# Sums of cached rows in one decoder step: 32 small matmuls a batch on TensorE in place of multiply-adds on VectorE and GpSimd

## The chip, the cores and the metric

The program runs on one core of one Trainium2 chip. The metric is the device time of one execution in microseconds (us), as the median of several runs. Engines are called TensorE (PE in the rows, with PEld for its weight loads), VectorE (DVE), ScalarE (ACT), GpSimd (POOL) and SyncE (SP, which here only issues transfers).

## What is computed

One inference step of a one-layer hybrid decoder, for a prompt of 512 tokens and for 8 sequences that decode 4 tokens each. The step has modulation vectors, an input projection, attention in three branches, a state-space mixer (SSD), an output projection and a mixture of 16 experts. The change concerns one piece of the attention of the 8 decoding sequences: 2048 cached key and value rows of each sequence are compressed, 32 rows to one, with one weight for each position.

```
def compress(rows, w_pos):
    b, l, g, d = rows.shape
    return jnp.einsum('bcjgd,j->bcgd', rows.reshape(b, l // CMP_BLOCK, CMP_BLOCK, g, d), w_pos)

rows = cache_cmp[layer, page_table].reshape(bd, PAST_LEN, 2, N_KV, HEAD_DIM)
kcmp = rmsnorm(compress(rows[:, :, 0], w_pos_k), g_k_cmp)
vcmp = compress(rows[:, :, 1], w_pos_v)
```

CMP_BLOCK is 32, a row has 128 numbers of key and 128 of value, and a sequence has 64 compressed rows.

## The kernel before

A sequence (a "batch" below, 0 to 7) is fetched by two gathers of 1 MB, `gcmp`, each of 128 partitions with 8 consecutive rows: four neighbouring partitions hold one block of 32 rows. `pool_batch(b)` makes the weighted sum over the 8 rows of a partition, the keys by one ScalarE and seven VectorE instructions (lines 492 and 494) and the values by four GpSimd instructions (lines 496 to 499), into the tile `psum` (an ordinary tile; the name is short for partial sums). Then TensorE adds each four partitions with the 0/1 mask `PM` in four matmuls, which write 32 PSUM partitions each, and ScalarE copies the result to `kvc`.

The eight batches are fillers among other work of the first part of the program, in an order written out by hand: `ORDER = "C f1 p f3 z c0 f1 c1 f4 q f1 c2 f2 c3 f1 e B f2"`. Here `fN` takes the next N fillers, which alternate `pool_batch(n)` and `ada_block(n + 4)` (32 small matmuls of the modulation vectors from 2 MB of weights, and 4 for a bias), and one `pool_batch` stands ahead of the list. C, z, q and B are quarters of the input projection; each is a loop over eight slices k in which ScalarE makes `wh` (line 339), VectorE makes `wl` (line 340) and TensorE runs 12 matmuls into the four `acc` tiles. `c0` to `c3` are the chunks of the SSD scan, with a chain of ScalarE (`lh`, `dec`), VectorE (`dec`, line 649) and TensorE; `p` is its convolution on VectorE (`ts`, lines 605 to 610).

The order on each engine is that of the framework's scheduler, which starts from the program's order and from its own estimate of when operands are ready; each engine then works its list strictly from the front. All gathers and 1 MB weight slices (`wada`, `wC`, `wF`, `wA`, `wB`) share seven slots (`SLOT`), so that a transfer starts when the reader of an earlier tile is done. SyncE issues the weight loads, GpSimd's queue the gathers. All matmuls are issued by the helper at line 97, so that their rows have this line and are told apart by their tiles.

Of the kernel before, what the change touches and what calls it, by code (L numbers as in the profile page):

```python
# [9 lines left out]
F32 = mybir.dt.float32  # L10
# [3 lines left out]
AF = mybir.ActivationFunctionType  # L14
OP = mybir.AluOpType
AX = mybir.AxisListType

P = 128
# [37 lines left out]
def hybrid_step(ctx: ExitStack, tc: tile.TileContext, a, o):  # L56
    nc = tc.nc
    V, S, G, T, SP = nc.vector, nc.scalar, nc.gpsimd, nc.tensor, nc.sync
# [7 lines left out]
    def nm(base):  # L66
        cnt[0] += 1
        return f"{base}_{cnt[0]}"

    def pool(name, side=None):  # L70
        cm = tc.tile_pool(name=name, bufs=1, reuse_waits="tile", side=side)
        p = cm.__enter__()
        return p, lambda: cm.__exit__(None, None, None)

    def const(shape, dt, name):
        return cst.tile(list(shape), dt, name=name, tag=name)

    def W(pl, shape, dt, tag, bufs=2):
        return pl.tile(list(shape), dt, name=nm(tag), tag=tag, bufs=bufs)

    psum = {}
# [8 lines left out]
    def PS(tag="ps"):  # L90
        return psum["pool"].tile([P, 512], F32, name=nm(tag), tag=tag, bufs=psum["tags"][tag])

    def SLOT(shape, dt=F32, name="st"):
        return st.tile(list(shape), dt, name=nm(name), tag="st8")

    def mm(out, lhsT, rhs, start=True, stop=True):
        T.matmul(out, lhsT, rhs, start=start, stop=stop)  # L97
# [83 lines left out]
    p1, close_p1 = pool("p1")  # L181
    ph, close_ph = pool("ph", "right")
# [52 lines left out]
    def brow(name, n, ap=None):  # L235
        t = const([P, n], F32, "bc_" + name)
        SP.dma_start(t, dram(a[name], 0, ap or [[0, P], [1, n]]))
        return t
# [23 lines left out]
    def block_mask(t, pattern, w, base=0):  # L262
        G.memset(t, 1.0)
        G.affine_select(t, t, pattern=pattern, compare_op=OP.is_ge, fill=0.0, base=base, channel_multiplier=1)
        G.affine_select(t, t, pattern=[[-s, n] for s, n in pattern], compare_op=OP.is_ge, fill=0.0,
                        base=w - 1 - base, channel_multiplier=-1)
# [19 lines left out]
    for k in range(KC):  # L286
        ps = PS("acc")
# [151 lines left out]
    with tc.issue_after(load_D(3)):  # L439
# [4 lines left out]
        wk8, wv8 = [brow(name, 8, [[0, 32], [8, 4], [1, 8]]) for name in ("w_pos_k", "w_pos_v")]  # L444
# [20 lines left out]
    ps = PS()  # L465
# [17 lines left out]

    def pool_batch(b):

        sums = W(ph, [P, 2, 256], F32, "psum")
        for h in range(2):
            gt = SLOT([P, 8, 256], name="gcmp")
            G.indirect_dma_start(out=gt.rearrange("p r c -> p (r c)"), out_offset=None, in_=cmp_rows,
                                 in_offset=bass.IndirectOffsetOnAxis(ap=idx[:, 2 * b + h:2 * b + h + 1], axis=0))  # L490
            y = sums[:, h, 0:P]
            S.activation(y, gt[:, 0, 0:P], AF.Copy, scale=wk8[:, 0:1])  # L492
            for i in range(1, 8):
                V.scalar_tensor_tensor(y, gt[:, i, 0:P], wk8[:, i:i + 1], y, op0=OP.mult, op1=OP.add)  # L494
            gv = gt[:, :, P:256]
            G.tensor_mul(gv, gv, wv8[:, :, None].to_broadcast([P, 8, P]))  # L496
            G.tensor_add(gv[:, 0:4, :], gv[:, 0:4, :], gv[:, 4:8, :])
            G.tensor_add(gv[:, 0:2, :], gv[:, 0:2, :], gv[:, 2:4, :])
            G.tensor_add(sums[:, h, P:256], gv[:, 0, :], gv[:, 1, :])
        ps = PS()  # L500
        for kv in range(2):
            for h in range(2):
                q = 32 * (2 * kv + h)
                mm(ps[q:q + 32, 0:P], PM, sums[:, h, kv * P:(kv + 1) * P])
        S.copy(kvc[:, b, :], ps[:, 0:P])


    PM = const([P, 32], F32, "PM")
    block_mask(PM, [[-4, 32]], 4)
    Wp = W(p1, [P, 2, NT, 16], F32, "Wp", 1)  # L510
    block_mask(Wp[:, 0], [[128, NT], [-32, 16]], 32)
    V.tensor_scalar_mul(Wp[:, 1], Wp[:, 0], wkp[:, 1:2])
    V.tensor_scalar_mul(Wp[:, 0], Wp[:, 0], wkp[:, 0:1])

    fillers = [f for n in range(8) for f in ((pool_batch, n), (ada_block, n + 4))]

    def fill(n):
# [7 lines left out]
    gts = mid.tile([P, NT, 32], F32, name="gts")  # L525
# [3 lines left out]
    ps = [PS(), PS()]  # L529
# [315 lines left out]
    for i, src in enumerate((us[:, 768:896], us[:, 1024:1152], kcv[:, 0:P])):  # L845
# [3 lines left out]
                        op=OP.add)  # L849
# [24 lines left out]
    ps = PS("sm")  # L874
# [13 lines left out]
    for t in range(NT):  # L888
# [6 lines left out]
        for hf in range(2):  # L895
            ps = PS("s")
# [59 lines left out]
    ps = PS("sm")  # L956
# [165 lines left out]
    ps = PS("sm")  # L1122
# [4 lines left out]
    ps = PS("sm")  # L1127
# [21 lines left out]
    ps = PS("sm")  # L1149
# [8 lines left out]
    for hb in range(2):  # L1158
        ps = PS("sm")
# [25 lines left out]
    ps = PS("sm")  # L1185
# [32 lines left out]
    ps = [PS("sm"), PS("sm")]  # L1218
# [17 lines left out]
    ps = [PS("sm"), PS("sm")]  # L1236
# [13 lines left out]
    for b2 in range(4):  # L1250
        ps = PS("sm")
# [28 lines left out]
    for g in range(2):  # L1280
# [7 lines left out]
                    op=OP.mult)  # L1288
# [23 lines left out]
    for i in range(4):  # L1312
        ph = PS("sm")
# [25 lines left out]
    ps = PS("s")  # L1339
# [9 lines left out]
    ps = PS("s")  # L1349
# [14 lines left out]
    for h in range(8):  # L1364
        for j in range(2):
            mm(pcs, kcT[:, h // 4, j, 112 - 16 * h:240 - 16 * h], QT[:, h, :], start=h == 0 and j == 0,
               stop=h == 7 and j == 1)
# [21 lines left out]
    ps = PS("s")  # L1389
# [4 lines left out]
    for t in range(NT):  # L1394
        ps = PS("s")
# [97 lines left out]
    for k in ko:  # L1493
        src = att if k < 4 else zy
        kk = k % 4
        ps = PS()
# [5 lines left out]
    ps = PS("pr")  # L1502
# [9 lines left out]
    ps = PS("pr")  # L1512
    for k in range(KC):
        T.transpose(ps[:, 32 * k:32 * k + 32], atS[:, k // 4, (k % 4) * P:(k % 4 + 1) * P], ident[0:NS, 0:NS])
    V.tensor_tensor(catS, ps[:, 0:256].rearrange("p (k c) -> p k c", c=NS), gcat[:, :, None].to_broadcast([P, KC, NS]),
                    op=OP.mult)
# [50 lines left out]
    ps = PS()  # L1567
# [8 lines left out]
    ps = PS()  # L1576
# [89 lines left out]
    ps = PS()  # L1666
# [97 lines left out]
    ps = PS()  # L1764
# [257 lines left out]
    with tc.issue_after(first), tc.issue_after(placed):  # L2022
        ps = PS("rt")
# [16 lines left out]
    with tc.issue_after(X[2]):  # L2040
        rts = {}
        for e in SEQ:
            ps = PS("rt")
# [8 lines left out]
    for i in range(NE + 1):  # L2052
        with tc.issue_after(X[3]):
# [4 lines left out]
            if n <= NE and n not in rts and n != XPOS:  # L2058
                ps = PS("rt")
# [54 lines left out]
def build(nc, shapes):  # L2114
    a, o = {}, {}
    for name in _INS:
        shape, dt = shapes[name]
        a[name] = nc.dram_tensor("in_" + name, shape, dt, kind="ExternalInput").ap()
    for name, shape in _OUTS:
        o[name] = nc.dram_tensor("out_" + name, shape, F32, kind="ExternalOutput").ap()  # L2120
    with tile.TileContext(nc, schedule_with_timeline_sim=True) as tc:
        hybrid_step(tc, a, o)
# [11 lines left out]
```

## Time and profile before

| | |
|---|---|
| median of 3 runs | 886.49 us (886.35 to 887.79) |
| profiled execution | 883.6 us, its span 881.9 us |
| TensorE busy in the span | 739.2 us (84%) |
| VectorE | 652.9 us (74%) |
| ScalarE | 394.3 us (45%) |
| GpSimd | 335.4 us (38%) |
| mean granted clock of TensorE | 0.903 of full |

The profiled execution has 1.7 us outside its span, and lies 2.9 us under the median. In rows of TensorE one f32 matmul leaves two records. A granted clock of 1.00 is 2.4 GHz, 0.50 is 1.2 GHz; a value between them is a mean over a stretch. The eight batches lie between 67 and 293 us of the span.

### The profile page before, as it was taken

The page shows a single profiled execution, that of the slowest core. Times are in us where ns is not written, and L with a number is a line of the kernel's source. Part 1 is how long each engine was busy: PE and PEld are TensorE (multiplying, and loading weights), DVE is VectorE, ACT ScalarE, POOL GpSimd, SP SyncE. Part 2 cuts the span into 40 slices and gives each one's busy share as a digit, 9 for nine tenths or more (in the row PEclk, how much of TensorE's full clock was granted, in tenths as well). Part 3 has the DMA queues.
Part 4 walks back from the last instruction along what each step waited for, and adds up shares of the span by engine and source line. Part 5 has one row for each costly group of instructions (what it writes and reads, how often), then busy time and mean ns, then how long its engine had stood idle before and what let it go on. Part 6 is the DMA issues. An engine that isn't in the chain of part 4 may idle for free.

```text
span 881.9 us, 14660 instructions
## 1 busy us (share of the span) xinstructions
PE 739.2 (84%) x5315; PEld 530.5 (60%) x5315; DVE 652.9 (74%) x1481; ACT 394.3 (45%) x894; POOL 335.4 (38%) x304
## 2 busy tenths in 40 slices
PE   5998868489969769998898898899589788898893
PEld 4666645376647555565557556677566557666662
DVE  5536899666795885745546645769899979989994
ACT  4324232332523423455244235422357557777781
POOL 1115565535481641100101301522335435466552
PEclk9999889779889759999999689999589989999997
DMA  8977474355641551113525032898388976876411
GB/s 290 376 227 278 149 282 166 144 191 188 242 144 48 194 207 53 44 44 149 191 100 191 1 96 82 262 338 312 122 319 279 286 239 212 282 235 210 115 32 21
DMA packets 67095, 161.85 MB, mean 184 GB/s; under 512 B 19005, under 2 KB 31238, under 8 KB 60622
## 3 DMA queue, kind: packets, MB, share of 16 engines
q1 hardware_dynamic: 56798, 115.54, 38.3%
q0 software_dynamic: 10224, 45.37, 15.7%
q8 instruction: 42, 0.69, 0.3%
q14 instruction: 31, 0.25, 0.1%
HBM read 153.48 MB, written 20.74 MB: 198 GB/s over the span
## 4 chain that ended last, share of the span: by engine, by line
PE 46%; DVE 32%; DMA 11%; issue 5%; ACT 4%; POOL 1%; SPq 1%; POOLq 0%; DVEq 0%; ACTq 0%
PE acc L97 16%; DVE wl L340 8%; PE smo L97 5%; DVE psum L494 4%; PE ps L97 4%; PE s L97 3%; DMA gcmp<-in_cache_cmp,idx 3%; PE sm L1008 3%; PE ot L97 3%; PE pt L805 3%; PE sm L97 2%; DMA gu<-in_w_up 2%; DMA wada<-in_w_ada 2%; DVE XL L1884 1%; DVE ts L607 1%
## 5 line engine op out<-in xcount | busy, mean ns | idle before, releaser
L494 DVE SCALAR_TENSOR_TENSOR psum<-gcmp,bc_w_pos_k,psum 128x128 f32<-128x128 f32 x112 | 62.9, 566 | 15.0 <-ACT psum L492 13.3
L97 PE MATMUL acc<-wl,XH 128*128 128x512 f32 x136 | 60.1, 442 | 11.5 <-DVE wl L340 7.7
L97 PE MATMUL acc<-wl,hH 128*128 128x512 f32 (+1 forms) x128 | 54.5, 429 | 18.1 <-DVE wl L340 18.1
L339 ACT CAST wh<-gu 128x512 fp32r<-128x512 f32 x88 | 51.3, 623 | 14.5 <-PE acc L97 12.1
L97 PE MATMUL acc<-wh,XH 128*128 128x512 f32 x136 | 55.4, 408 | 0.4 <-ACT XH L1883 0.4
L97 PE MATMUL acc<-wh,XL 128*128 128x512 f32 x136 | 54.8, 403 | 0.7 <-DVE XL L1884 0.7
L340 DVE TENSOR_TENSOR wl<-gu,wh 128x512 fp32r<-128x512 f32 x66 | 51.6, 812 | 1.0 <-ACT wh L339 0.9
L97 PE MATMUL acc<-wh,hL 128*128 128x512 f32 (+1 forms) x128 | 52.1, 410 | 0.0
L802 ACT ACTIVATE psb<-s,amx 128x128 f32<-128x128 f32 (+3 forms) x64 | 33.8, 528 | 40.7 <-DVE amx L800 33.1
L1032 POOL DMA_INDIRECT gsel<-in_cache_sel,idx x16 | 16.8, 1052 | 88.7 <-PE smo L97 75.5
L800 DVE TENSOR_REDUCE amx<-s 128x1 f32<-128x128 f32 (+3 forms) x64 | 30.8, 483 | 19.8 <-PE s L97 11.2
L97 PE MATMUL acc<-wh,hH 128*128 128x512 f32 (+1 forms) x128 | 43.5, 416 | 2.3 <-ACT wh L339 2.2
L97 PEld LDWEIGHTS acc<-wl,hH 128*128 128x128 f32 x128 | 27.5, 214 | 26.0 <-DVE wl L340 20.0
L340 DVE TENSOR_TENSOR wl<-dn,wh 128x512 fp32r<-128x512 f32 x39 | 38.3, 1001 | 5.8 <-ACT wh L339 5.7
L97 PEld LDWEIGHTS acc<-wl,XH 128*128 128x128 f32 x136 | 26.3, 194 | 25.8 <-DVE wl L340 15.5
L340 POOL TENSOR_TENSOR wl<-gu,wh 128x512 fp32r<-128x512 f32 x22 | 31.3, 1458 | 21.7 <-ACT wh L339 21.6
L97 PE MATMUL s<-KT,QT 128*128 128x384 f32 (+3 forms) x128 | 38.2, 384 | 1.1 <-DVE qa L823 0.8
L1929 POOL DMA_INDIRECT out_y_prompt<-yo,gir x16 | 28.3, 1770 | 26.5 <-DVE yo L1923 8.3
L97 PE MATMUL ps<-wada,scT 128*32 128x128 f32 x768 | 37.1, 280 | 1.1 <-DMA wada<-in_w_ada 0.5
L805 PE MATMUL pt<-ident,psb 128*128 128x128 f32 x160 | 32.4, 305 | 6.0 <-ACT psb L802 5.9
L339 ACT CAST wh<-dn 128x512 fp32r<-128x512 f32 x52 | 31.8, 620 | 12.1 <-PE acc L97 10.7
L496 POOL TENSOR_TENSOR gcmp<-gcmp,bc_w_pos_v 128x1024 f32<-128x1024 f32 x16 | 31.7, 1982 | 12.8 <-DMA gcmp<-in_cache_cmp,idx 12.8
(790 smaller groups left out, 2177.7 us busy)
## 6 DMA issues: line engine op xcount, KB each, us to landing
wada<-in_w_ada SPq DMA_DIRECT2D x24, 1024.0 KB
dn<-in_w_down SPq DMA_DIRECT2D x12, 1024.0 KB
gu<-in_w_gate SPq DMA_DIRECT2D x21, 512.0 KB
gu<-in_w_up SPq DMA_DIRECT2D x21, 512.0 KB
gux<-in_w_gate SPq DMA_DIRECT2D x11, 512.0 KB
gux<-in_w_up SPq DMA_DIRECT2D x11, 512.0 KB
wt<-in_cache_win SPq DMA_DIRECT2D x4, 1024.0 KB
wout<-in_w_out SPq DMA_DIRECT2D x4, 1024.0 KB
```

Of the source, the lines that this page charges most:

```text
L97: T.matmul(out, lhsT, rhs, start=start, stop=stop)
L339: S.copy(wh[:, 0:n], w)
L340: (eng or V).tensor_sub(wl[:, 0:n], w, wh[:, 0:n].bitcast(F32))
L494: V.scalar_tensor_tensor(y, gt[:, i, 0:P], wk8[:, i:i + 1], y, op0=OP.mult, op1=OP.add)
L496: G.tensor_mul(gv, gv, wv8[:, :, None].to_broadcast([P, 8, P]))
L607: V.scalar_tensor_tensor(c, xpad[:, k, j:j + 512], cwT[:, j, k:k + 1], c, op0=OP.mult, op1=OP.add)
L800: V.tensor_reduce(mx, ps[:, 0:n], axis=AX.X, op=OP.max, negate=True)
L802: S.activation(pb[:, 0:n], ps[:, 0:n], AF.Exp, bias=mx, accum_out=sm[:, h:h + 1])
L805: T.transpose(pt[:, c * P:(c + 1) * P], pb[:, c * P:(c + 1) * P], ident)
L1008: T.transpose(ps[:, j * P:(j + 1) * P], src(j), ident)
L1032: G.indirect_dma_start(out=t.rearrange("p r c -> p (r c)"), out_offset=None, in_=sel_rows, in_offset=bass.IndirectOffsetOnAxis(ap=idx[:, 2 ...
L1929: G.indirect_dma_start(out=y_p, out_offset=bass.IndirectOffsetOnAxis(ap=gi, axis=0), in_=yo, in_offset=None, bounds_check=511, oob_is_err= ...
```

## The change

`pool_batch` no longer makes sums on VectorE and GpSimd. Sixteen masks `PW` are made once: `PM` times the weight of row i, for keys and for values. For each batch TensorE multiplies each of the 8 rows of a partition with its mask and accumulates in PSUM: 8 rows by keys and values by two gathers are 32 matmuls where there were 4. Both gathers of a batch are issued ahead of its first matmul, and both slots are held until its last. Nothing else is edited, and GpSimd keeps only the gathers' issues of this work.

```
     def pool_batch(b):
 
-        sums = W(ph, [P, 2, 256], F32, "psum")
+        gts = []
         for h in range(2):
             gt = SLOT([P, 8, 256], name="gcmp")
             G.indirect_dma_start(out=gt.rearrange("p r c -> p (r c)"), out_offset=None, in_=cmp_rows,
                                  in_offset=bass.IndirectOffsetOnAxis(ap=idx[:, 2 * b + h:2 * b + h + 1], axis=0))
-            y = sums[:, h, 0:P]
-            S.activation(y, gt[:, 0, 0:P], AF.Copy, scale=wk8[:, 0:1])
-            for i in range(1, 8):
-                V.scalar_tensor_tensor(y, gt[:, i, 0:P], wk8[:, i:i + 1], y, op0=OP.mult, op1=OP.add)
-            gv = gt[:, :, P:256]
-            G.tensor_mul(gv, gv, wv8[:, :, None].to_broadcast([P, 8, P]))
-            G.tensor_add(gv[:, 0:4, :], gv[:, 0:4, :], gv[:, 4:8, :])
-            G.tensor_add(gv[:, 0:2, :], gv[:, 0:2, :], gv[:, 2:4, :])
-            G.tensor_add(sums[:, h, P:256], gv[:, 0, :], gv[:, 1, :])
+            gts.append(gt)
         ps = PS()
-        for kv in range(2):
-            for h in range(2):
-                q = 32 * (2 * kv + h)
-                mm(ps[q:q + 32, 0:P], PM, sums[:, h, kv * P:(kv + 1) * P])
+        for i in range(8):
+            for kv in range(2):
+                for h in range(2):
+                    q = 32 * (2 * kv + h)
+                    mm(ps[q:q + 32, 0:P], PW[:, kv, i, :], gts[h][:, i, kv * P:(kv + 1) * P], start=i == 0, stop=i == 7)
         S.copy(kvc[:, b, :], ps[:, 0:P])
...
     block_mask(PM, [[-4, 32]], 4)
+    PW = W(p1, [P, 2, 8, 32], F32, "PW", 1)
+    for kv, w8 in enumerate((wk8, wv8)):
+        V.tensor_tensor(PW[:, kv], PM[:, None, :].to_broadcast([P, 8, 32]), w8[:, :, None].to_broadcast([P, 8, 32]),
+                        op=OP.mult)
```

The scheduler orders the changed program anew. The first place is TensorE's list in the projection q, where batch 5 is to be summed. The matmuls into the four `acc` tiles are full ones with 128 output partitions, and those into `ps` write 32 partitions and belong to the batch. Before:

```order
L97 MATMUL acc_1908<-wh_2013,hH 128x512
L97 MATMUL acc_1908<-wl_2014,hH 128x512
L97 MATMUL acc_1908<-wh_2013,hL 128x512
L97 MATMUL acc_1909<-wh_2013,hH 128x512
L97 MATMUL ps_2141<-psum_2112,PM 32x128 x2
L97 MATMUL acc_1909<-wl_2014,hH 128x512
L97 MATMUL acc_1909<-wh_2013,hL 128x512
L97 MATMUL acc_1910<-wh_2013,hH 128x512
```

The same place in TensorE's list after the change:

```order
L97 MATMUL acc_1926<-wh_2011,hH 128x512
L97 MATMUL ps_2134<-gcmp_2130,PW_837 32x128
L97 MATMUL acc_1926<-wl_2012,hH 128x512
L97 MATMUL ps_2134<-gcmp_2132,PW_837 32x128
L97 MATMUL acc_1926<-wh_2011,hL 128x512
L97 MATMUL ps_2134<-gcmp_2130,PW_837 32x128
L97 MATMUL acc_1927<-wh_2011,hH 128x512
L97 MATMUL ps_2134<-gcmp_2132,PW_837 32x128
L97 MATMUL acc_1927<-wl_2012,hH 128x512
```

Where two small matmuls stood between full ones in a pair, single small ones now alternate with full ones. Between 75 and 296 us of the span before, and in the same part of the program after, 52 small matmuls stand alone between full ones where 5 did, and the runs of small matmuls between full ones number 83 where there were 39; the other batches stand in blocks.

The second place is GpSimd's list after the first batch: the gathers (line 489), the window norms (line 552 before, 549 after) and the sums. Before:

```order
L489 DMA gcmp_1311<-in_cache_cmp,idx 128x2048
L489 DMA gcmp_1325<-in_cache_cmp,idx 128x2048
L499 TENSOR_TENSOR psum_1233<-gcmp_1248 128x128
L496 TENSOR_TENSOR gcmp_1311<-gcmp_1311,bc_w_pos_v 128x8x128
L552 TENSOR_TENSOR wino<-wino,bc_g_k_win 128x4x64 x2
L489 DMA gcmp_1751<-in_cache_cmp,idx 128x2048
L497 TENSOR_TENSOR gcmp_1311<-gcmp_1311 128x4x128
L498 TENSOR_TENSOR gcmp_1311<-gcmp_1311 128x2x128
```

GpSimd's list at the same gathers after the change:

```order
L489 DMA gcmp_1241<-in_cache_cmp,idx 128x2048
L489 DMA gcmp_1319<-in_cache_cmp,idx 128x2048
L489 DMA gcmp_1321<-in_cache_cmp,idx 128x2048
L549 TENSOR_TENSOR wino<-wino,bc_g_k_win 128x4x64 x2
L489 DMA gcmp_1762<-in_cache_cmp,idx 128x2048
L489 DMA gcmp_1764<-in_cache_cmp,idx 128x2048
L651 TENSOR_TENSOR xdw_1604<-xt_1534,bc_d_skip 128x512
```

The gathers no longer stand behind sums of an earlier gather, so that only the release of a slot holds them. That release now comes from TensorE: in SyncE's list the first slice of `wA`, which is issued into a slot of batch 3, waited for VectorE, ScalarE and GpSimd before, and waits for TensorE after.

## Rows read from the trace of the kernel before

**Rows 1.** The page: busy us (share) x instructions of each engine.

```profile
PE 739.2 (84%) x5315; PEld 530.5 (60%) x5315; DVE 652.9 (74%) x1481; ACT 394.3 (45%) x894; POOL 335.4 (38%) x304
```

**Rows 2.** Chain of work that ended last, 75 to 296 us, shares by line.

```profile
by line: PE acc L97 18.8%; DVE psum L494 17.8%; DMA gcmp<-in_cache_cmp,idx 13.2%; PE ps L97 10.9%; DVE ts L607 5.1%; DVE wl L340 4.9%; issue 3.8%; DVE dec L649 3.6%; DVE qa L718 2.6%; DVE sp_mp L155 1.6%; DVE ts L605 1.5%; DVE rsq_yk L119 1
```

**Rows 3.** 75 to 296 us: length, busy of PE, PEld, DVE, ACT, POOL; clock; DMA.

```profile
75.00:296.00 221.00, 178.75 (x1526) 132.31 (x1524) 176.35 (x338) 73.09 (x196) 121.94 (x108) 0.88 0.47 170
```

**Rows 4.** Waits of TensorE, 75 to 296 us: us in total, times, longest.

```profile
PE acc L97 <- DVE wl L340: 19.1, 7, 8.7
PE ps L97 <- DVE dec L649: 14.1, 3, 11.1
PE ps L97 <- DVE psum L494: 3.3, 2, 1.9
```

**Rows 5.** Tile `gcmp`: duration ns min/median/max, first and last start.

```profile
L494 DVE SCALAR_TENSOR_TENSOR psum<-gcmp,bc_w_pos_k,psum x112: 246/351/2635, 75.8 to 270.2; 128x128 f32<-128x128 f32 x112
...
L496 POOL TENSOR_TENSOR gcmp<-gcmp,bc_w_pos_v x16: 1894/1939/2417, 75.4 to 256.6; 128x1024 f32<-128x1024 f32 x16
L497 POOL TENSOR_TENSOR gcmp<-gcmp x16: 1262/1284/2401, 77.4 to 259.7; 128x512 f32<-128x512 f32 x16
```

**Rows 6.** Stretch: length, busy of PE and PEld on tile `wada`, clock.

```profile
206.40:208.50 2.10, 1.96 (x64) 1.69 (x64) 1.00 0.00 0
```

**Rows 7.** The page, costliest groups: small matmuls of `wada`, mean 280 ns.

```profile
L97 PE MATMUL ps<-wada,scT 128*32 128x128 f32 x768 | 37.1, 280 | 1.1 <-DMA wada<-in_w_ada 0.5
```

**Rows 8.** Timeline of TensorE, start and duration us: small matmuls between full ones.

```profile
138.72 0.39 PE L97 MATMUL acc<-wl,hH 128*128 128x512 f32 x1
138.96 0.39 PE L97 MATMUL acc<-wh,hL 128*128 128x512 f32 x1
139.27 0.41 PE L97 MATMUL ps<-wF,hsT 128*32 128x128 f32 x4
139.62 0.33 PE L623 MATMUL ps<-ident,xx 128*128 128x128 f32 x1
...
217.28 0.41 PE L97 MATMUL ps<-wA,hsT 128*32 128x128 f32 x2
217.61 0.39 PE L97 MATMUL ps<-dta,LT 128*128 128x8 f32 x2
```

**Rows 9.** Stretches of 2 us: first and last of 35 with clock under 0.99.

```profile
82.00:84.00 2.00, 1.57 (x10) 0.88 (x9) 1.97 (x4) 1.96 (x5) 1.60 (x2) 0.87 0.00 0
...
266.00:268.00 2.00, 2.00 (x7) 1.57 (x6) 1.08 (x5) 0.22 (x1) 0.00 (x0) 0.55 0.60 122
```

**Rows 10.** Timeline of TensorE: idle before it and its releaser in brackets.

```profile
124.70 0.80 PE L97 MATMUL acc<-wl,hH 128*128 128x512 f32 x1 [4.69 <-DVE wl L340]
172.00 0.69 PE L97 MATMUL ps<-xt,dec 128*128 128x64 f32 x2 [11.14 <-DVE dec L649]
263.97 0.79 PE L97 MATMUL acc<-wl,hH 128*128 128x512 f32 x1 [8.70 <-DVE wl L340]
```

**Rows 11.** Chain of work that ended last: start us, us, what.

```profile
67.44 7.89 DMA gcmp<-in_cache_cmp,idx
...
155.54 8.59 DMA gcmp<-in_cache_cmp,idx
...
243.43 6.96 DMA gcmp<-in_cache_cmp,idx
...
256.95 5.83 DVE qa L718 x4
```

**Rows 12.** Timeline of SyncE: the first issue of `wA`.

```profile
178.99 0.90 SPq L171 DMA_DIRECT2D wA<-in_w_in  x2
```

**Rows 13.** Timeline of TensorE: last small matmuls, then the stage's end.

```profile
295.00 0.42 PE L97 MATMUL ps<-bada,e 12*32 12x128 f32 x8
...
300.28 0.66 PE L898 MATMUL s<-ident,qhl 128*128 128x128 f32 x2 [4.86 <-DVE ssn L838]
```

**Rows 14.** Timeline of VectorE: products over 128 partitions by 256.

```profile
150.36 0.74 DVE L553 TENSOR_TENSOR wino<-wino,rsq_zk 128x256 f32<-128x256 f32 x2
```

## The prediction

> **What bounds the kernel now.** I read the page first: TensorE is busy for 84% of the span and VectorE for 74% [rows 1], so neither can be left out. The change acts where the batches lie, so I then took the chain of work that ended last between 75 and 296 us. There TensorE's two lines hold 18.8% and 10.9%, but VectorE's key sums (line 494) hold 17.8% and the landing of gathers 13.2% [rows 2]. The chain hops between the two engines, and the busy times say why: in these 221 us TensorE works 178.75 and VectorE 176.35 [rows 3]. So TensorE idles only 42.3 us there. The waits name VectorE for nearly all of it: `wl` 19.1, `dec` 14.1, the key sums themselves 3.3 [rows 4]. That is the ceiling for what a relieved VectorE can give back, and every microsecond added to TensorE is paid against it.
>
> A second loss hangs on this idling. I cut the stretch into pieces of 2 us; in 35 of the 110 the granted clock is under 0.99 (first and last shown) [rows 9]. In each piece I took TensorE's busy time times (1 − clock), the time that full clock would have saved; the sum over the 35 is 18.4 us. Such pieces follow idle stretches: after 8.70 us of idle the matmuls of 263.97 start at the lower level, 1.2 GHz (0.50 of full; the piece from 266 us still has 0.55) [rows 9, 10].
>
> **What the change removes.** VectorE loses 112 instructions. Their median is 351 ns but the longest takes 2635 [rows 5]; with the page's total, 62.9 us for these 112, VectorE falls from 176 to about 114 us in the stretch. GpSimd loses four instructions a half batch, the first two of them 1.94 and 1.28 us [rows 5], so over 50 us by these two alone, and ScalarE 16 copies. GpSimd (121.94 us) and ScalarE (73.09) are far from full [rows 3], so I book nothing for them. The two new products that make `PW` (128 partitions by 256) cost 0.37 us each by the pair at 150.36 [rows 14]; they stand before the first gather lands at 75 us and lie beside its 7.89 us [rows 11]: nothing. Without that cover they cost 0.7.
>
> **What it adds on TensorE, in blocks.** A pooled batch is 32 small matmuls, of the same shape as an `ada_block` (128 contraction rows, 32 output partitions, 128 columns): 64 records in 1.96 us [rows 6], so 31 ns a record. Eight batches are 15.7 us; the 4 matmuls a batch that go (64 records) were 2.0, so +13.7. The last batch I take out again: at the end of the stage TensorE is done at 295.4 and next has work at 300.28, after 4.86 us of waiting for VectorE [rows 13], which covers 2.0. Without that cover the term is 13.7 instead of **+11.7**.
>
> The Trainium skill would make more of this: "TensorE: Matmul & The Clock Gate", section "Measured speedup vs the span model", has a packed group of tiles last as long as one matmul plus some 4 ns for each further tile. With 0.280 us for one of these records [rows 7], four packed ones would by that last 0.292 us, an estimate; a batch is 8 such groups for each of two records, and eight batches, 128 groups, come to 37.4 us in place of 15.7. The 1.96 us for 64 records [rows 6] stands against it.
>
> **What it adds in singles.** The order after shows 52 small matmuls that alternate with full ones. What does one cost? At 138.72 and 138.96 full matmuls follow at 0.24 us; then a run of four small records takes from 139.27 to 139.62, 0.35 us, and the full one ahead of it holds for 0.31 instead of 0.24. At 217.28 two records take 0.33 [rows 8]. So a run costs about 0.34 for itself and 0.09 at its borders, nearly whatever its length: 0.43 us, where 31 ns a record would give 0.06. The 47 added singles cost 47 × 0.37 = **+17.4 us** beyond their block price; the other small runs between full ones go from 34 to 31: **−1**. The bounds: nothing (if the price is a modelled end and not a stall) and 47 × 0.43 = 20; I keep near the upper, where the rows lie.
>
> A rule of the Trainium skill speaks against the change here: "TensorEngine Tiling (Array Packing)", section "Key Properties", says that changing the tiling mode drains the engine. The 0.33 to 0.35 us runs agree with it; by a flat rate instead the sum would be 17.4 lower (a rival below).
>
> **What it gives back: idle time.** Of the 42.3 us, waits stay which have nothing to do with the key sums. The three waits for `dec` are 14.1 in all [rows 4], and 11.14 of it is one, at 172.00 [rows 10], behind a gather of 8.59 us at 155.54 and its sums [rows 11]; the other 3 stay. The 8.70 at 263.97 [rows 10] lies half behind a gather of 6.96 us and half behind four scalings of `qa`, 5.83 us on the chain [rows 11]; some 4 stay. With 4 for the small ones: 11 stay.
>
> New waits come in, since TensorE works strictly in order and now is the one that needs the gathers. The second gather of batch 2 stands ahead of the projection z in TensorE's list, with about 4 us of other work between its slot's release and its first matmul, against a landing of 7 to 8.6 us [rows 11]: 3.5. And the slot of the first `wA` slice, which SyncE issues at 178.99 [rows 12], is now released by TensorE behind batch 3 instead of by three engines ahead of it. Its 1 MB lands in about 8 to 9 us if it takes as long as a gather's 1 MB; one `ada_block` and batch 4 (2 × 2) cover about half: 5.5. Queued behind it in SyncE are the second `wA` slice and the `wada` slices; they wait with it, and TensorE's first matmul of q waits for all. So 9 new, bounded by 0 (other work covers it) and some 29 (rival C).
>
> Idle goes from 42.3 to 11 + 9 = 20: **−22.3 us**. Of the 18.4 us at lower clock I expect half to stay with half of the idling: **−9**.
>
> **The sum.** +11.7 + 17.4 − 1 − 22.3 − 9 = −3.2. From the profiled execution's own 883.6 that is 880.4; that execution lay 2.9 under the median of the runs, so I predict 883. After 296 us nothing is edited, but the scheduler orders it anew (its changes between widths of matmul go from 192 to 202 up to the mixture of experts): I put this at 0 ± 4.
>
> **Rivals.**
> B: a switch between small and full matmuls has no price of its own. For it: durations in a row are modelled ends. Against it: a run of two records and one of four take 0.33 and 0.35 us, the same for half the work [rows 8]. The 16.4 us fall away: 864 own, 867 as a median.
> D: the relief is whole. VectorE at 114 of 221 us runs ahead of TensorE all the time, idle falls to 8 and the lower clock to 3. For it: every large wait names VectorE [rows 4]. Against it: gathers are 13.2% of the chain by themselves [rows 2]. That is 12 + 6 us more: 862 own, 865 as a median.
> C, on the slower side: TensorE stands before the gathers. Batches 2, 4 and 5 wait for a landing in full, three times 7.8 us by the three of the chain [rows 11], 23.4 in place of 3.5. For it: the gathers wait for slots that TensorE itself releases, in order, and GpSimd's queue now issues them one behind another. Against it: GpSimd no longer works sums ahead of a gather's issue. That gives 900 own, 903 as a median. It decides once the waits for gathers pass the 3.5 us by more than 5.
> That the change does not do what it says can be set aside: the lists of all engines show the sums gone.
>
> **How the numbers follow.** My forecast has 0.46, with 875 to 891 as its own range (lower bound: half the price of the singles, 8.7; upper: both covers gone, 2.7, and 5 us of further waits). B has 0.13, D 0.20, C 0.21. Less than 0.2% of the time, 1.8 us, can't be told from no change. Of the forecast's 0.46, 0.23 lies under 884.7, 0.12 within, 0.11 above; B and D are faster, C slower: faster 0.56, same 0.12, slower 0.32. The range leaves out a tenth at each end: 864, so that B and D are inside, to 901, where C begins to be outside.
>
> **What the profile after would show.** Right: 512 records of `ps` from `gcmp` and `PW`, in blocks at about 1.96 us for 64 and as singles with about 0.4 us between full matmuls; the 11.14 us wait for `dec` gone; waits of TensorE for gathers and for `wA` of about 9 us; VectorE near 590 us in the whole span; fewer pieces at the lower clock. Wrong: full matmuls beside singles at a cadence of about 0.27 (B); TensorE idle under 10 us in the stretch (D); waits of over 8 us for gathers (C). The prediction would fail altogether if the new order after 296 us costs or gives more than 4 us, since I priced it from nothing but a count.

## The result, and the profile after

The changed kernel takes 854.01 us as the median of 4 runs (852.42 to 854.83), the kernel before 886.42 (884.81 to 887.79): a ratio of 0.9651, with a 95% interval of 0.9622 to 0.968. The direction was right and the size was not: 883 was forecast with 864 as the lower end, so the gain of 32.4 us was not in the range.

To see where the time went I use one mark in both traces, the start of the first matmul of `s` from `KT` (the scores of the attention, behind everything that the change touches). It lies at 320.1 us before and at 308.8 after. So 11.3 us were won ahead of the mark, and 19.9 us behind it, where no line of code was edited: 563.5 us of the profiled execution lie behind the mark before, 543.6 after (852.42 − 308.8). The mark's row before and after:

```profile
320.10 0.44 PE L97 MATMUL s<-KT,QT 128*128 128x128 f32 x2
```

```profile
308.83 0.44 PE L97 MATMUL s<-KT,QT 128*128 128x128 f32 x2
```

The page of the changed kernel, busy time of each engine, answers to [rows 1]:

```profile
PE 746.3 (88%) x5763; PEld 530.7 (62%) x5763; DVE 567.5 (67%) x1371; ACT 391.1 (46%) x878; POOL 263.4 (31%) x240
```

VectorE has lost 85 us in the whole span, not the 63 of its removed instructions. The stretch from 75 us to the mark (length; busy of PE, PEld, DVE, ACT, POOL; clock; DMA), and TensorE's waits in it, answer to [rows 3, 4]:

```profile
75.00:308.80 233.80, 211.00 (x2041) 150.16 (x2039) 115.02 (x295) 75.77 (x195) 56.92 (x64) 0.93 0.52 188
```

```profile
PE acc L97 <- ACT wh L339: 7.3, 1, 7.3
PE s L895 <- DVE QT L105: 6.5, 2, 4.0
PE ps L97 <- DVE dec L646: 1.9, 2, 1.5
```

The same view of the kernel before, to its own mark:

```profile
75.00:320.10 245.10, 193.84 (x1590) 144.10 (x1588) 197.02 (x406) 80.74 (x212) 134.72 (x128) 0.85 0.50 178
```

TensorE works 17.2 us more and idles 22.8 us instead of 51.3. The 19.1 us of waits for `wl` and the 11.14 us for `dec` are gone; the wait of 7.3 us is new. Its row names `wh`, but ScalarE itself stood there for a transfer, as its timeline shows:

```profile
172.99 0.62 ACT L339 CAST wh<-wA 128x512 fp32r<-128x512 f32 x1 [7.42 <-DMA wA<-in_w_in]
```

Stretches of 2 us with a clock under 0.99 are 9 between 76 and 286 us, and cost 5.4 us by the measure of [rows 9], instead of 18.4. To the mark the same measure gives 11.3 us after and 25.2 before. A pooled batch in a block costs what an `ada_block` costs (length, busy of PE and PEld on tile `PW`, of DVE, clock), as [rows 6] said:

```profile
80.80:82.90 2.10, 1.95 (x64) 1.69 (x64) 0.00 (x0) 1.00 0.00 0
```

Singles look like this on TensorE's timeline (start and duration in us), a pair every 0.76 us where a block and unmixed full matmuls would take 0.06 and 0.24:

```profile
212.48 0.41 PE L97 MATMUL ps<-gcmp,PW 128*32 128x128 f32 x2
212.82 0.49 PE L97 MATMUL acc<-wh,hH 128*128 128x512 f32 x1
213.24 0.41 PE L97 MATMUL ps<-gcmp,PW 128*32 128x128 f32 x2
```

### The profile page after: what moved, and what is told of

It reads as the page before. It is cut to its first block, busy times and chain, and to the rows that moved or that the text cites. A ratio compares the mean times of both kernels' runs of the same rounds, so it can differ in the third digit from the quotient of the medians.

```text
span 850.7 us, 15349 instructions
## 1 busy us (share of the span) xinstructions
PE 746.3 (88%) x5763; PEld 530.7 (62%) x5763; DVE 567.5 (67%) x1371; ACT 391.1 (46%) x878; POOL 263.4 (31%) x240
## 5 line engine op out<-in xcount | busy, mean ns | idle before, releaser
L339 ACT CAST wh<-gu 128x512 fp32r<-128x512 f32 x88 | 51.3, 619 | 10.4 <-PE acc L97 9.8
L340 DVE TENSOR_TENSOR wl<-gu,wh 128x512 fp32r<-128x512 f32 x66 | 54.1, 847 | 0.7 <-ACT wh L339 0.6
L97 PE MATMUL acc<-wl,hH 128*128 128x512 f32 (+1 forms) x128 | 50.6, 400 | 0.0
L97 PE MATMUL acc<-wh,hL 128*128 128x512 f32 (+1 forms) x128 | 49.2, 388 | 0.0
L97 PE MATMUL ps<-wada,scT 128*32 128x128 f32 x768 | 45.3, 293 | 3.2 <-DVE modT L409 1.3
L489 POOL DMA_INDIRECT gcmp<-in_cache_cmp,idx x16 | 17.1, 1066 | 85.3 <-PE ps L97 72.5
L1029 POOL DMA_INDIRECT gsel<-in_cache_sel,idx x16 | 17.4, 1087 | 83.3 <-PE smo L97 74.1
L97 PEld LDWEIGHTS ps<-wada,scT 128*32 128x32 f32 x768 | 31.2, 117 | 15.4 <-issue 9.5
L340 DVE TENSOR_TENSOR wl<-wA,wh 128x512 fp32r<-128x512 f32 x8 | 5.4, 690 | 52.7 <-ACT wh L339 52.7
L97 PEld LDWEIGHTS acc<-wl,XH 128*128 128x128 f32 x136 | 26.3, 193 | 22.3 <-DVE wl L340 11.8
L340 POOL TENSOR_TENSOR wl<-gu,wh 128x512 fp32r<-128x512 f32 x22 | 32.6, 1513 | 18.9 <-ACT wh L339 18.7
L1926 POOL DMA_INDIRECT out_y_prompt<-yo,gir x16 | 30.1, 1879 | 22.1 <-DVE yo L1920 12.2
L802 PE MATMUL pt<-ident,psb 128*128 128x128 f32 x160 | 32.4, 302 | 3.5 <-ACT psb L799 3.5
```

The lines of the kernel that those rows point to most:

```text
L339: S.copy(wh[:, 0:n], w)
L340: (eng or V).tensor_sub(wl[:, 0:n], w, wh[:, 0:n].bitcast(F32))
L802: T.transpose(pt[:, c * P:(c + 1) * P], pb[:, c * P:(c + 1) * P], ident)
L1029: G.indirect_dma_start(out=t.rearrange("p r c -> p (r c)"), out_offset=None, in_=sel_rows, in_offset=bass.IndirectOffsetOnAxis(ap=idx[:, 2 ...
L1926: G.indirect_dma_start(out=y_p, out_offset=bass.IndirectOffsetOnAxis(ap=gi, axis=0), in_=yo, in_offset=None, bounds_check=511, oob_is_err= ...
```

## The experiments

Theory 1 is rival D of the prediction: VectorE's load was what TensorE waited for, and TensorE's own time is the bound once it is gone. Two questions were open: is it VectorE's own 112 instructions that count or GpSimd's work, and is the gain behind the mark the change's or the scheduler's? In all experiments "mark" is the first matmul of `s` from `KT`, and times behind it are those of the profiled execution.

**Blocks.** The changed kernel with a higher priority for all small matmuls:

```
     def ada_block(n):
...
+        with tc.high_priority(offset=300):
             for k in range(KC):
...
     def pool_batch(b):
...
+        with tc.high_priority(offset=300):
             for i in range(8):
...
```

> The changed kernel with its small matmuls (pooled batches and modulation blocks) issued at a higher priority, so that 4 of them stand alone between full ones in the stretch where 52 did. Mark: start of the first matmul of s from KT, 308.8 us in the changed kernel, 320.1 before; what lies behind the mark takes 543.6 us and 563.5. Theory 1 (TensorE's own time is the bound of the stretch, and a single costs 0.46 us as an alternating pair of 0.76 us shows): 48 singles less give 22 us, the mark at 287 to 292. Rival (the singles fill time in which TensorE would wait for wh and wl anyway): TensorE's idle time grows by as much as its busy time falls, the mark at 304 to 310. Behind the mark any order may come, 540 to 565.

830.98 us, ratio 0.9397 (0.9329 to 0.9464). The mark is at 296.3, between the two, nearer to theory 1. TensorE's busy time to the mark falls from 211.00 to 193.11, 17.9 us for 48 singles or 0.37 each; idle time grows from 22.8 to 28.2. Its waits for transfers come to 9.4 us, where the changed kernel has 8.4 (7.3 for `wA`, 0.7 for `wF`, 0.4 for a gather), and one wait for `ts` of VectorE is 5.4 us instead of 1.3. The waits for transfers:

```profile
PE ps L97 <- DMA wA<-in_w_in: 5.1, 1, 5.1
PE ps L97 <- DMA wada<-in_w_ada: 4.3, 2, 3.5
```

**Only the keys, only the values, on TensorE.** In each, one half of the old `pool_batch` stays: GpSimd's four instructions in the first (its matmuls are shown), the ScalarE and VectorE ones in the second.

```
+        for h in range(2):
+            mm(ps[64 + 32 * h:96 + 32 * h, 0:P], PM, sums[:, h, 128:256])
         for i in range(8):
-            for kv in range(2):
-                for h in range(2):
-                    q = 32 * (2 * kv + h)
-                    mm(ps[q:q + 32, 0:P], PW[:, kv, i, :], gts[h][:, i, kv * P:(kv + 1) * P], start=i == 0, stop=i == 7)
+            for h in range(2):
+                mm(ps[0 + 32 * h:32 + 32 * h, 0:P], PW[:, 0, i, :], gts[h][:, i, 0:128], start=i == 0, stop=i == 7)
```

> Keys summed on TensorE with weighted masks, values still on GpSimd as before. Theory 1 (VectorE was what TensorE waited for): VectorE loses its 63 us, TensorE gets half the added matmuls and 5 singles, so idle time under 20 us and the mark at 285 to 295. Rival (GpSimd's 80 us were the trouble, by holding the slots until its sums are done): idle time stays at 30 us or more and the mark at 303 or later.

851.2 us, ratio 0.9598 (0.9545 to 0.9651); mark 304.8, idle time 229.80 − 193.94 = 35.9. That is the rival's outcome, but the mark can't be held against theory 1 in full. Its matmuls write only two groups of 32 output partitions in turn, and 32 records take as long as the 64 of a whole batch in four groups (columns as for the block above):

```profile
86.00:88.20 2.20, 1.94 (x32) 1.67 (x32) 0.00 (x0) 1.00 0.03 7
```

In eight batches that is 15.5 us for half the matmuls, some 8 us more than theory 1 counted with. The idle time speaks for the rival without this.

> Values summed on TensorE with weighted masks, keys still on VectorE. Theory 1 (VectorE's load is the bound): the 112 multiply-adds stay; if they run at their shortest row, 0.25 to 0.27 us, once GpSimd is silent, they cost 30 us in place of 63, so half of the relief: idle time 25 to 35 us, the mark at 303 to 312. Rival (GpSimd's work is the trouble, by itself and by slowing VectorE): the whole relief comes here, idle time under 20 us, the mark at 285 to 295.

843.94 us, ratio 0.9538 (0.9485 to 0.959); mark 300.1, idle time 30.7, VectorE busy 150.44 us to the mark with all 112 multiply-adds still there, which take 41.5 us. This is theory 1's idle time but a better mark than it allowed, though its blocks have the same price as those with the keys (1.94 us for 32 records). It is also better than the mark of the whole change, but that has 52 singles where by the trace only some 4 are left here; the run with blocks, at 296.3, is the fairer neighbour. GpSimd had to be looked at by itself.

**One sum left out.** Two kernels take work out of the kernel before and add nothing to TensorE; the first leaves out 7 of 8 value rows, the second 7 of 8 key rows.

```
-            gv = gt[:, :, P:256]
-            G.tensor_mul(gv, gv, wv8[:, :, None].to_broadcast([P, 8, P]))
-            G.tensor_add(gv[:, 0:4, :], gv[:, 0:4, :], gv[:, 4:8, :])
-            G.tensor_add(gv[:, 0:2, :], gv[:, 0:2, :], gv[:, 2:4, :])
-            G.tensor_add(sums[:, h, P:256], gv[:, 0, :], gv[:, 1, :])
+            S.activation(sums[:, h, P:256], gt[:, 0, P:256], AF.Copy, scale=wv8[:, 0:1])
```

> The kernel before without the value sums: ScalarE copies one weighted row in the place of GpSimd's four instructions, so 7 of 8 value rows are left out of the sum; TensorE gets nothing added and VectorE keeps all 112 key multiply-adds. Theory 2 (GpSimd's elementwise work lengthened VectorE's, so that a silent GpSimd relieves VectorE too): VectorE's busy time to the mark falls from 197 to 145 to 155 us, the 112 instructions from 62.9 to about 42, and the mark comes to 292 to 302. Rival (GpSimd costs only its own time, which was hidden): VectorE stays over 185 us and the mark within 5 us of 320.1.

817.56 us, ratio 0.9305 (0.9253 to 0.9357). To the mark:

```profile
75.00:274.40 199.40, 179.54 (x1591) 135.68 (x1589) 149.62 (x409) 85.40 (x228) 53.17 (x64) 0.91 0.61 220
```

VectorE does every one of its instructions and needs 149.62 us instead of 197.02. The 112 multiply-adds are a part of that (busy us, mean ns; before, then here):

```profile
L494 DVE SCALAR_TENSOR_TENSOR psum<-gcmp,bc_w_pos_k,psum 128x128 f32<-128x128 f32 x112 | 62.9, 566 | 15.0 <-ACT psum L492 13.3
```

```profile
L494 DVE SCALAR_TENSOR_TENSOR psum<-gcmp,bc_w_pos_k,psum 128x128 f32<-128x128 f32 x112 | 38.6, 358 | 14.1 <-ACT psum L492 12.4
```

Their median hardly moves, 351 ns before [rows 5] and 348 here, but the longest falls from 2635 to 1014. In the kernel before, the longest one ends (85.53) just behind the GpSimd product that starts during it (83.47 + 1.90 = 85.37):

```profile
82.90 2.63 DVE L494 SCALAR_TENSOR_TENSOR psum<-gcmp,bc_w_pos_k,psum 128x128 f32<-128x128 f32 x1
```

```profile
83.47 1.90 POOL L496 TENSOR_TENSOR gcmp<-gcmp,bc_w_pos_v 128x1024 f32<-128x1024 f32 x1
```

The mark comes 45.7 us earlier, more than theory 2 had asked.

```
-            for i in range(1, 8):
-                V.scalar_tensor_tensor(y, gt[:, i, 0:P], wk8[:, i:i + 1], y, op0=OP.mult, op1=OP.add)
```

> The kernel before without VectorE's 112 key multiply-adds: 7 of 8 key rows are left out of the sum; GpSimd's value sums stay. VectorE loses the 62.9 us that the forecast counted with. Theory 1 (the forecast's: these instructions are the load that counts): idle time of TensorE to the mark under 30 us, and the mark at 295 to 303 in spite of 15 more singles. Theory 2 (GpSimd goes on lengthening the rest of VectorE's work, whose instructions keep their long durations, such as 0.50 us for dec): VectorE falls by 50 to 60 us, no more, idle time 30 to 40 us, and the mark at 303 to 310.

822.79 us, ratio 0.9377 (0.9316 to 0.9438). VectorE falls by 44.3 us to 152.69, less than the 62.9 taken out, and the mark to 291.6, 28.5 us earlier; idle time 26.0. So theory 1 has the idle time, and the mark lies 3.4 us below its range; neither theory has VectorE's fall. What is left on VectorE became slower: 152.69 us, where the kernel before has 197.02 − 62.9 = 134.1 for it. VectorE's groups to the mark, without key sums (busy us and mean ns behind the bar):

```profile
L605 DVE SCALAR_TENSOR_TENSOR ts<-xx,cw,ts 128x512 f32<-128x512 f32 x18 | 21.5, 1195 | 0.2
L647 DVE SCALAR_TENSOR_TENSOR dec<-dec,dt,cbm 128x128 f32<-128x128 f32 x32 | 17.9, 620 | 8.8 <-ACT dec L644 8.7
L340 DVE TENSOR_TENSOR wl<-wA,wh 128x512 fp32r<-128x512 f32 x8 | 9.1, 1153 | 18.9 <-ACT wh L339 18.9
```

and in the changed kernel, where GpSimd makes no sums:

```profile
L604 DVE SCALAR_TENSOR_TENSOR ts<-xx,cw,ts 128x512 f32<-128x512 f32 x18 | 13.3, 741 | 0.2
L646 DVE SCALAR_TENSOR_TENSOR dec<-dec,dt,cbm 128x128 f32<-128x128 f32 x32 | 9.1, 347 | 12.3 <-ACT dec L643 12.2
...
L340 DVE TENSOR_TENSOR wl<-wA,wh 128x512 fp32r<-128x512 f32 x8 | 5.4, 690 | 52.7 <-ACT wh L339 52.7
```

The same three groups take 48.5 us beside GpSimd's sums and 27.8 without them; in the kernel before it was 38.5.

**Order alone.** The kernel before with the two `high_priority` lines of the run with blocks around its own small matmuls; no operation is changed.

> The kernel before with the same higher priority on its small matmuls: all work as before, only the scheduler's order differs, in the stretch and behind it. Theory 1: the mark within 5 us of 320.1, since VectorE's load is untouched. Behind the mark, where 2131 of TensorE's 3118 matmuls stand in the same order as before: if the 20 us that the changed kernel gained there came from a better order by chance, this order too should move that part by 5 to 20 us, one way or the other; if they came from the stretch itself (transfers that start earlier), it stays within 3 us of 563.5.

852.46 us, ratio 0.9625 (0.9581 to 0.9669), as fast as the changed kernel. The mark stands at 320.1, where it was; all of the gain lies behind it, 533.3 us in place of 563.5. From the mark to the output projection's first matmul, the kernel before and this one:

```profile
320.10:549.30 229.20, 207.44 (x1623) 132.70 (x1624) 133.16 (x381) 98.23 (x271) 31.88 (x41) 0.92 0.28 97
```

```profile
320.10:528.70 208.60, 194.54 (x1625) 127.81 (x1625) 126.68 (x365) 95.84 (x266) 30.02 (x41) 0.95 0.31 109
```

In the kernel before, the same matmuls (some records are missing in either) take 12.9 us more of TensorE's busy time, 6.8 of them by the measure of [rows 9] for the lower granted clock, and 7.7 us more of idling. The rest of the 30.2 us, 9.6, lies behind the output projection's first matmul. A smaller step of priority gives a third order:

> The kernel before with a smaller step of priority for its small matmuls (100 in place of 300), which gives a third order: 1921 of the 3118 matmuls behind the stretch stand in the order of the kernel before. Theory (behind the stretch the kernel before has an order that happens to be slow; most orders take 533 to 547 us there): 530 to 550 us behind the mark, and the mark within 5 us of 320, 4 later for its 12 added singles at most. Rival (only the priority of 300 finds a good order): 555 to 570 us behind the mark.

851.04 us, ratio 0.9583 (0.9567 to 0.96); mark 317.3 and 535.5 us behind it, as the theory said.

**A barrier in both.** One line at the end of the stretch, in the kernel before and in the changed one:

```
             steps[step]()
+    tc.strict_bb_all_engine_barrier()
     for j in range(4):
```

> The kernel before with one barrier of all engines at the end of the stretch, so that the scheduler orders what follows from a like state in both kernels. Its partner is the changed kernel with the same barrier: of TensorE's 3118 matmuls behind the stretch 2955 stand in the same order in the two, where 2323 did without barriers. Theory (what the change won behind the stretch was the scheduler's new order and not the change): the two differ by less than 5 us behind the mark, first matmul of s from KT, where the kernels without barriers differ by 19.9. Rival (the change itself speeds up what follows): 15 to 20 us between them there again.

869.98 us, ratio 0.9792 (0.977 to 0.9814); mark 325.3 and 546.2 behind it.

> The changed kernel with the same barrier; its order has 14 small matmuls alone between full ones where the changed kernel has 52, and its partner 6. Theory: the mark lies 18 to 26 us ahead of its partner's (the 11.3 us of the changed kernel and 38 singles less at 0.37 each, the fall of TensorE's busy time for each in the run with blocks, less some idle time), and that is all of the difference of the two times. Rival: over 30 us, with 15 or more behind the mark.

844.03 us, ratio 0.9503 (0.9486 to 0.9521); mark 295.0 and 549.8 behind it. The gain of 26.0 us lies ahead of the mark (30.3, above the 18 to 26 expected); behind it the pair differs by 3.6 us, the other way.

**Twice the matmuls.** The run with blocks, each batch's loop written twice.

> The run with blocks with every pooled batch's 32 matmuls made twice, the second over the first; the result stays the same. Theory 1 (TensorE's own time is the bound of the stretch): 512 further records at 1.96 us per 64 are 15.7 us, and 5 more singles 1.9, so the mark goes from 296.3 to 309 to 315. Rival (TensorE's idle time of 28 us in that stretch covers them): the mark moves by less than 6 us.

856.86 us, ratio 0.9655 (0.9639 to 0.9671), its profiled execution 7.7 us under that. The mark moves from 296.3 to 314.7, 18.4 us, so theory 1 has it. TensorE's busy time rises by more than was expected, from 193.11 to 217.09, and idle time takes up 5.6 us of these 24.0 (28.2 to 22.6): some three quarters of the work added to TensorE are paid at the mark.

**Priority 100 in the changed kernel.** Beside the third order of the kernel before.

> The changed kernel with priority 100, the partner of the kernel before with the same (mark 317.3, 535.5 us behind it); 16 singles where the partner has 17. Theory: the mark 16 to 30 us ahead of the partner's, at 288 to 301, as between the two with priority 300 (23.8) and the two with a barrier (30.3); behind the mark 530 to 550 us, on either side of the partner's by chance of order. Rival (pooling on TensorE is worth only the 11 us that the plain order shows): the mark at 304 to 309.

841.29 us, ratio 0.9579 (0.9532 to 0.9625); mark 298.4. The runs of the kernel before that were made beside it had a median of 879.05, those of its partner 887.8, and the two ratios are alike though the marks lie 18.9 us apart. So I ran both again on one chip:

> The kernel before with priority 100, again, beside its partner on one chip. Theory (the change is worth 11 to 30 us in the stretch, and the part behind the mark follows the order): 849 to 855 us, the mark at 317, 535 us behind it.

> The changed kernel with priority 100, beside its partner. Theory: the mark 16 to 20 us ahead of the partner's, and 4 to 9 us of it lost behind the mark to this pair's orders (542.8 against 535.5 in the two calls), so 8 to 16 us faster in all. Rival (with a like order the change is worth nothing, as the two ratios 0.958 say): within 3 us.

851.91 and 841.71 us, ratios 0.9659 (0.9618 to 0.97) and 0.9529 (0.9485 to 0.9572): 10.2 us, with marks at 317.8 and 299.8. In this pair 14.1 us of the 18.0 are lost again behind the mark (530.4 against 544.5) in the profiled executions, where 4 to 9 had been expected.

**The first slot released earlier.** The run with blocks with `for h` as the outer loop:

```
-            for i in range(8):
-                for kv in range(2):
-                    for h in range(2):
+            for h in range(2):
+                for i in range(8):
+                    for kv in range(2):
```

> The run with blocks with the 32 matmuls of a batch in another order: all 16 of the first gather, then all of the second, so that the first slot comes free about 1 us earlier, and 2 singles in place of 4. If the slots held by TensorE cost the 9.4 us of waits for the transfers of wA and wada in the run with blocks (mark 296.3), an earlier release takes 1 to 3 us from them: the mark at 292 to 296. If these waits hang on something else, they stay, and the mark within 1 us. Behind the mark 530 to 550 us.

827.58 us, ratio 0.9448 (0.9388 to 0.9508); mark 297.0. The waits for `wA` and `wada` are down to 0.9 us, as a held slot would have it, but the mark is where it was: a block now takes longer (columns as for the block above).

```profile
80.70:84.20 3.50, 3.29 (x64) 3.02 (x64) 0.00 (x0) 1.00 0.02 7
```

> The version with blocks again, beside the one that releases the first slot early. Theory: 1.95 us for 64 records where four column groups take turns, 9.4 us of waits for the transfers of wA and wada; the mark at 296, the same within 2 us as the other version's.

> The version with all 16 matmuls of the first gather ahead of those of the second. Theory: its blocks take 3.29 us for 64 records, since only two column groups take turns, 1.3 us more a batch, and under 1 us of waits for wA and wada are left; the two cancel, so the mark within 2 us of the other version's, and the times differ by what the order behind the mark gives, 5 us or less.

835.58 and 832.57 us, ratios 0.9459 (0.9408 to 0.9509) and 0.9446 (0.9404 to 0.9488), marks at 296.4 and 296.6. The waits for `wA` and `wada` are 7.0 us in the first (9.4 expected) and 0.9 in the second. The intervals overlap, so neither is shown to be the faster; both beat the changed kernel (0.9651).

## Why the prediction was wrong

**The part behind the stretch.** The step that failed most is "I put this at 0 ± 4" for what follows 296 us. It came out at −19.9, of the 31.2 us between the two profiled executions. The forecast had said that it fails altogether if this happens, and that the term was priced from nothing but a count. The runs show that this is the list's doing: the kernel before in two other orders, with every operation unchanged, wins 28.0 and 30.2 us there, and with a like order forced by the barrier the gain there is not to be seen. The thirteen other programs have 529 to 550 us behind the mark; only the kernel before has 563.5. Its order was a slow one, and all edits tried here ended it. The same program twice differs there by up to 5.8 us, so smaller differences mean nothing. Which step loses the time in that order stays open; up to the output projection I only saw lower clock and more idling.

**The relief of VectorE.** "VectorE falls from 176 to about 114 us" and, of GpSimd, "I book nothing for them" were mis-sized. To the mark VectorE lost 82.0 us (197.02 to 115.02): 62.9 with the 112 instructions, and 19.1 because those that stayed became shorter. The run without value sums shows that GpSimd's sums had lengthened them: without these sums alone VectorE needs 47.4 us less, 24.3 of it in the 112 multiply-adds and 23.1 in the rest. The row that pointed there was shown, 246 to 2635 ns for one shape [rows 5]; the forecast quoted the median and the longest and did not ask what made the difference. By the Trainium skill, "GPSIMD Engine Reference", section "1. Specifications", GpSimd shares its interfaces to SBUF with VectorE and collides with VectorE instructions that run in a 2-port performance mode or have two SBUF inputs. The multiply-adds and `wl` have two SBUF inputs, and the 62.9 us of the multiply-adds beside GpSimd's sums against 38.6 without them agree with it. So do two products of VectorE with one input in PSUM, `cbm` from `ps` and `UT`: at 225.07 and 256.75 us of the kernel before they run while GpSimd has a product of 1.9 us under way, and last 0.29 and 0.28 us, as they do in the run without value sums (mean 281 ns). No run here tests the 2-port mode. GpSimd's sums also kept a slot until they were done; how much of the 45.7 us is that was not separated.

**Idle time and clock.** Idle to the mark fell by 28.5 us; the forecast's was 22.3 and 2.0 for the covered last batch. The clock gave 13.0 instead of 9. So the stretch came to −11.3 where −3.2 was forecast, 4 us from each. That lies between the forecast and rival D, the whole relief, which had 18 us more than the forecast; D's sign, idle time under 10 us, did not show (14.6 us up to 284.7, against 42.3 before). That D's 865 us is the figure next to the measured 854 is luck: the part behind the mark brought it there. What stays of idle was foreseen in its main part: the wait for `wA` was 7.3 us (5.5 forecast), behind a slot that TensorE releases. The wait before z was 0.7 for `wF` and 0.4 for a gather instead of 3.5, so rival C found nothing.

**What TensorE pays.** This held. Blocks cost 1.95 us (1.96 forecast). A single cost 0.37 us in the run with blocks, as forecast, and 0.46 in the regular pairs above; rival B, no price for a switch, is out. With the clock's share to the mark, 25.2 − 11.3 = 13.9, the forecast's terms give 13.7 + 17.4 − 1 − 13.9 = 16.2 us, and TensorE's busy time rose by 17.2.

**What the change is worth.** In the stretch 11.3 us in the plain order, 23.8 with priority 300, 18.0 with 100, 30.3 with the barrier. The plain order has 47 singles more than its partner, which goes with the smallest gain; among the other three the number of singles does not set the order (16 against 17 with priority 100, 14 against 6 with the barrier). In the whole, at like priorities, 21.5, 10.2 and 26.0 us; the 32.4 that were measured hold an order's luck besides.

## What to carry to other kernels

Where a scheduler writes the order, an edit changes the list far behind itself: before a gain is put down to the edit, run the kernel before in another order or two, and see how far that alone moves the time. An engine off the critical path can still be the cost: look at the spread of one instruction's duration, not its median, when another engine works beside it. Small matmuls belong in blocks: with the pooled batches and the modulation blocks kept together the mark came 12.5 us earlier.

## What the runs showed of the hardware

Two things I had not expected. The same 64 records of 128 by 32 took 1.95 us where four groups of 32 output partitions took turns, and 3.29 us where only two did, at a granted clock of 1.00 in both; the two runs with half of the sums on TensorE, where two groups take turns as well, took 1.94 us for 32. And elementwise sums on GpSimd made VectorE's work in the same stretch a third longer (149.62 us to 197.02) with the same instructions on VectorE.
